# W2's Strassen block sums in DRAM and ScalarE squares, in one encoder layer

## Chip, cores and metric

The kernel runs on one core of a Trainium2 chip. The metric is the device time of one execution in microseconds (us); lower is better. The engines are named TensorE (PE in the profile; PEld are its weight loads), VectorE (DVE), ScalarE (ACT), GpSimd (POOL) and SyncE (SP, which only issues DMAs here).

## What is computed

One encoder layer on x of 2048 tokens by 1024 channels, all in float32. Two mixers read the same normalised input: dilated window attention (8 heads of 64) and a gated unit; a common output projection follows. Then comes the part that most of this document is about, the feed-forward network with hidden width 4096:

```python
x = x + rms_norm(mix, g_post_mix)
h = rms_norm(x, g_pre_ffn)
f = jnp.square(jax.nn.relu(h @ w_ff1)) @ w_ff2
return x + rms_norm(f, g_post_ffn)
```

w_ff1 is 1024 x 4096, w_ff2 is 4096 x 1024.

## The kernel before, in words

Every float32 product is made of three: each operand is split into a high part (a cast on ScalarE) and a low part (a subtraction on VectorE), and `mm3` (lines 92 to 94) adds low x high, high x low and high x high in PSUM. `split_sbuf` (lines 54 to 60) makes such a pair: line 59 is the cast, line 60 the subtraction; lines 56 and 57 are the same with a gain, for w_ff1.

The kernel has three stages. `stage1` norms x, projects it with w_in and writes the attention's operands to DRAM. `stage2` is the attention; it is left as it is. `stage3` has the output projection, in a loop over 16 token tiles written out by hand, and then the feed-forward network.

The network runs in 4 passes (`ps`) of 512 tokens, and in each pass over 8 groups (`g`, NG = 8) of 512 hidden channels. A group does this:

* First layer: 4 tiles f0 to f3 of 128 hidden channels by 512 tokens, 8 pieces of w_ff1 each (`ff1_first` does f0 and f1 together, `ff1_one` f2 and f3). `squares` (lines 934 to 940) applies Relu on ScalarE (line 937) and squares the result, in two halves of 256 tokens, on GpSimd (line 940).
* Second layer: Strassen's scheme in Winograd's form, 7 products instead of 8, over 2 x 2 blocks of tokens (256 each) by output columns (512 each) by hidden channels; the 512 hidden channels are two blocks, each of two tiles, p = 0 and p = 1. `operands` forms the four sums of hidden blocks on GpSimd (lines 1094, 1095, 1100, 1102) and the seven pairs fh, fl. p = 0 needs f0 and f2, p = 1 needs f1 and f3.
* `load2` (line 972) loads four tiles of 128 x 1024 of w_ff2, and `differences` (lines 983 to 985) and `second2` (line 1123) form its four block sums on GpSimd, anew in each pass; `first2` and `second2` make pairs wh, wl of the seven W2 operands. The first four operands (1, 2, 6, 5) have 8 buffers of their own; the other three (7, 3, 4) use the buffers of w_ff1's pieces after f3 is done.
* `ff2` runs the 7 products in the order of `CHAIN` for the row tiles m = 0 and 1. Sums that belong to several output blocks go on in the same PSUM bank: after product 1, VectorE adds the bank to `acc` (line 1154), and product 6 continues in this bank, so it has to wait for that addition. The order 1, 2, 6, 5, 7, 3, 4 uses the banks 1, 0, 1, 2, 1, 2, 1.
* `load1` loads and splits the next group's pieces of w_ff1.

TensorE, ScalarE, VectorE, GpSimd and SP each work through their own queue in order. Within the network and stage 1 that order is made by the scheduler of the language (program order is the priority among what is ready); in the loop of the output projection it is the written order for all five, and in stage 2 for TensorE and ScalarE. In that loop the loads of the first group's W2 tiles come at i = 13 and their differences at i = 16.

The first stage works with pools of buffers: x's tiles have the tag `xt` (4 buffers of 128 x 1024), the transposed tiles that go to DRAM the tag `ht` (2 buffers). `rstd_pow` (lines 98, 99) computes norm factors on GpSimd. `gates` is the gated unit for two token blocks; `prep` norms and transposes a tile of 128 tokens.

Of the kernel before, what the change touches and what calls it, by code (L numbers as in the profile page):

```python
# [9 lines left out]
F32 = mybir.dt.float32  # L10
F32R = mybir.dt.float32r
BF16 = mybir.dt.bfloat16
AF = mybir.ActivationFunctionType
ALU = mybir.AluOpType
# [3 lines left out]
P = 128  # L18
S = 2048
D = 1024  # L20
# [137 lines left out]
def stage1(tc, c, a, oh):  # L158
    nc = tc.nc
    with ExitStack() as ctx:  # L160
# [53 lines left out]
        def wload(col0):  # L214
            return [wpiece(col0, kc) for kc in range(8)]
# [108 lines left out]
        def gates(ws, hs, b0, w_next, between=None):  # L324

            v = do_zv(ws, hs[0])
            if between:
                between()
            w = wload(w_next)
            v2 = do_zv(ws, hs[1])  # L330
            do_sgu(v, b0)
            do_qk(w, hs[0], b0, c.qd, 0.125)
            do_sgu(v2, b0 + 1)
            return w


        hs = [new_h(), new_h()]
# [16 lines left out]
            nc.sync.dma_start(f32(c.vd[r0:r0 + P]), zeros)  # L354
        w = gates(wz, hs, 0, 0, consts)
        do_qk(w, hs[1], 1, c.qd, 0.125)
        w = wload(512)
        do_qk(w, hs[0], 0, c.kd, None)
        nh = [prep_all(2)]
        wz = wload(2048)  # L360
        do_qk(w, hs[1], 1, c.kd, None)
        nh.append(prep_all(3))
        hs = nh


        w = gates(wz, hs, 2, 0)
        zctx.close()
        do_qk(w, hs[1], 3, c.qd, 0.125)
        w = wload(512)
        for e in range(2):  # L370
            do_qk(w, hs[e], 2 + e, c.kd, None)
        w = wload(1024)
        do_v(w, hs[0], 2)
        c.wu = wload(1536)
        c.qk = c.qctx.enter_context(tc.tile_pool(name="s2q", bufs=2, side="right"))
        c.fk = c.fctx.enter_context(tc.tile_pool(name="s2fk", bufs=2, side="right"))
# [512 lines left out]
def stage3(tc, c, a, out):  # L889
# [4 lines left out]
    with ExitStack() as ctx:  # L894
# [39 lines left out]
        def squares(b, m, raw):  # L934

            raw[m] = fp.tile([P, 512], F32, name="rf", tag=f"rf{m}")
            nc.scalar.activation(raw[m], b, AF.Relu)  # L937
            for e in range(2):
                sl = raw[m][:, 256 * e:256 * e + 256]
                nc.gpsimd.tensor_tensor(sl, sl, sl, ALU.mult)  # L940

        def ff1_mm(b, h, ws, m, kc):
            wh, wl = ws[kc]
# [17 lines left out]
                    yield  # L961
            squares(b, m, raw)

        def load2(g):

            raws = []
            for p in range(2):
                two = []
                for e in range(2):
                    r = fp.tile([P, D], F32, name="w2r", tag="w2r", bufs=4)  # L970
                    k = 4 * g + 2 * e + p
                    nc.sync.dma_start(r, w2[k * P:(k + 1) * P, :])
                    two.append(r)
                raws.append(two)
            return raws

        def differences(raws):

            ts = []
            for r1, r2 in raws:  # L980
                t1 = fp.tile([P, 512], F32, name="t1", tag="t1", bufs=2)
                t2 = fp.tile([P, 512], F32, name="t2", tag="t2", bufs=2)
                nc.gpsimd.tensor_tensor(t1, r1[:, 512:], r1[:, :512], ALU.subtract)
                nc.gpsimd.tensor_tensor(t2, r2[:, 512:], t1, ALU.subtract)
                nc.gpsimd.tensor_tensor(r1[:, 512:], r2[:, 512:], r1[:, 512:], ALU.subtract)
                ts.append((t1, t2))
            return ts

        def start2(g):
            raws = load2(g)  # L990
            return raws, differences(raws)

        with ExitStack() as octx:
            orp = octx.enter_context(tc.tile_pool(name="s3r", bufs=4, side="right"))
# [23 lines left out]
            load_attn(nc, c, 1)  # L1018
            parts[0] = load_part(0)
            halves(0)  # L1020
            raws, ws0, raw0 = [], [], {}
            early = {7: 3, 8: 3, 9: 3, 11: 1, 12: 1, 13: 1, 14: 1, 15: 1}
            for i in range(18):
                old = 0 <= i - 1 < 16
                if 0 <= i - 3 < 4:
                    turned(xs[i - 3], h[0], h[1], i - 3)
                if i + 1 < 16:
                    halves(i + 1)
                if 0 <= i - 2 < 16:
                    nc.sync.dma_start(rows(i - 2), parts[i - 2])  # L1030
                    if i - 2 < 4:
                        rs2 = meansq(parts[i - 2])
                if old:
                    rs = meansq(parts[i - 1])
                if i < 16:
                    xs[i] = load_x(i)
                if i + 1 < 16:
                    parts[i + 1] = load_part(i + 1)
                if i == 7:
                    unit = ff1_first(h, ws0, raw0)  # L1040
                if i == 11:
                    unit = ff1_one(h, ws0, 2, raw0)
                if i == 13:
                    v0 = load2(0)
                if i == 16:
                    v0 = v0, differences(v0)
                for n in range(2):
                    if i < 16:
                        b = pm.tile([P, 512], F32, name="mo", tag="mm3")
                        ns = slice(n * 512, (n + 1) * 512)  # L1050
                        mh, ml = ops[i]
                        for kc in range(4):
                            mm3(nc, b, mh[:, kc, :], ml[:, kc, :], *c.wo[4 * n + kc], kc == 0, kc == 3)
                    for _ in range((early.get(i, 0) + 1 - n) // 2):
                        next(unit, None)
                    if old and n == 0:
                        r = parts[i - 1]
                        nc.vector.scalar_tensor_tensor(r, r, rs, gmix, ALU.mult, ALU.mult)
                        nc.vector.tensor_tensor(r, r, xs[i - 1], ALU.add)
                    if 0 <= i - 2 < 4 and n == 1:  # L1060
                        nc.scalar.activation(xs[i - 2], parts[i - 2], AF.Copy, scale=rs2)
                    if i < 16:
                        nc.vector.tensor_tensor(parts[i][:, ns], b, parts[i][:, ns], ALU.add)
                if i % 2 == 0 and i + 2 < 16:
                    product(nc, c, i // 2 + 1)
                    if i + 4 < 16:
                        load_attn(nc, c, i // 2 + 2)
                for _ in range(len(raws)):
                    ws0.append(piece_split(nc, c, raws.pop(0), c.gffn[:, len(ws0):len(ws0) + 1]))
                if 1 <= i < 5:  # L1070
                    raws = [piece_load(nc, c, w1[kc * P:(kc + 1) * P, 0:512]) for kc in range(2 * i - 2, 2 * i)]
# [4 lines left out]
        with ExitStack() as fctx:  # L1076
# [26 lines left out]
                op(3, a12)  # L1103
                op(4, a22)

            def w2op(pool, src):
                wh = pool.tile([P, 512], F32R, name="wh", tag="wh")
                wl = pool.tile([P, 512], F32R, name="wl", tag="wl")
                split_sbuf(nc, src, wh, wl)
                return wh, wl  # L1110

            def first2(v, ws):
                raws, ts = v
                for n in (1, 2, 6, 5):
                    for p in range(2):
                        src = {1: raws[p][0][:, :512], 2: raws[p][1][:, :512], 6: ts[p][1], 5: ts[p][0]}[n]
                        ws[n, p] = w2op(w2p, src)

            def second2(v, ws):
                raws, ts = v  # L1120
                for p in range(2):
                    r2 = raws[p][1]
                    nc.gpsimd.tensor_tensor(r2[:, :512], r2[:, :512], ts[p][1], ALU.subtract)
                for n in (7, 3, 4):
                    for p in range(2):
                        src = {7: raws[p][0][:, 512:], 3: raws[p][1][:, 512:], 4: raws[p][1][:, :512]}[n]
                        ws[n, p] = w2op(c.wp, src)

            def load1(g):
                return [piece(nc, c, w1[kc * P:(kc + 1) * P, g * 512:(g + 1) * 512], scale=c.gffn[:, kc:kc + 1])  # L1130
# [30 lines left out]
            for ps in range(4):  # L1161
# [33 lines left out]
                    return x1  # L1195

                for g in range(NG):
                    if ps == g == 0:
                        raw, v = raw0, v0
                    else:  # L1200
                        raw, v = {}, start2(g)
                    fs, w2s = {}, {}
                    first2(v, w2s)
                    if not ps == g == 0:
                        for _ in ff1_first(h, ws, raw):
                            pass
# [6 lines left out]
                    last = g == NG - 1  # L1213
                    if last and ps < 3:
                        nx = [next_in(i) for i in range(4)]
                    second2(v, w2s)
                    if not last or ps < 3:
                        ws = load1((g + 1) % NG)

# [40 lines left out]
def scratch(c, mk):  # L1260

    c.vd = mk("vd", [S + 2 * VPAD, NH, 2 * DH])
    c.qd = [[mk(f"qd{e}{m}", [P, S]) for m in range(4)] for e in range(2)]
    c.kd = [[mk(f"kd{e}{m}", [P, S]) for m in range(4)] for e in range(2)]
    c.hd = mk("hd", [16, P, 8, P], F32)
    c.sd = mk("sd", [16, P, 512], F32)
    c.sgd = mk("sgd", [16, P, 4, P], F32)
    c.part = mk("part", [S, D], F32)
    c.tab = mk("tab", [NH, 3 * 384], F32)
    c.bt = mk("bt", [NH, P, 3 * 384 + 1], F32)  # L1270
    c.od = mk("od", [512, S], F32)
    c.rd = mk("rd", [NH, S], F32)


# [62 lines left out]
```

## Time and profile before

| | us |
|---|---|
| median of 2 runs | 2805.06 (2803.39 to 2806.74) |
| the profiled execution, its time | 2790.99 |
| its span, first to last instruction | 2789.0 |
| TensorE busy (products) | 2452.9 (88%) |
| VectorE busy | 1850.3 (66%) |
| ScalarE busy | 1285.5 (46%) |
| GpSimd busy | 1134.3 (41%) |

Products are pipelined, so that a busy TensorE still contains time at the lower clock. Mean granted clock of the span: 0.924 of full speed. Stage 3's projection ends and the network's Strassen products begin at 1086.65.

### The profile page before, as it was taken

What the parts mean: (1) busy time and instruction counts of PE and PEld (TensorE: products, weight loads), DVE (VectorE), ACT (ScalarE), POOL (GpSimd) and SP (SyncE); (2) the same over time, 40 slices, a digit from 0 to 9 for tenths busy, and PEclk for the clock granted to TensorE, in tenths of its full rate; (3) what the DMA queues carried; (4) which work ended last, traced back from release to release, by engine and by line L of the source; (5) the groups of instructions that cost most, each with busy time, mean ns of one, the idle gap of its engine ahead of it and who ended that gap; (6) DMA issues with size and microseconds to landing.
All of it is one profiled execution on the core that took longest, in us unless ns stands there. A gap on an engine that the chain in (4) does not pass through costs nothing. (4 is left out here: it accounts for less than half of the span.)

```text
span 2789.0 us, 33978 instructions
## 1 busy us (share of the span) xinstructions
PE 2452.9 (88%) x11207; PEld 2002.8 (72%) x11207; DVE 1850.3 (66%) x3222; ACT 1285.5 (46%) x2837; POOL 1134.3 (41%) x1161
## 2 busy tenths in 40 slices
PE   8999999998998896888888898888789888888887
PEld 6787888887887675766766676676577667667766
DVE  4535335777665378677668767768776777776676
ACT  5334223776777344443345434335533434433433
POOL 4112006333321336454345435435534544543552
PEclk9999999999999998998998998899889899989989
DMA  7654557878866585222224222224322224322221
GB/s 257 198 185 133 177 166 216 206 184 198 192 152 175 179 280 212 84 83 77 83 71 164 83 76 91 68 83 151 99 78 69 91 73 143 107 74 84 74 86 42
DMA packets 232916, 365.51 MB, mean 131 GB/s; under 512 B 39201, under 2 KB 122660, under 8 KB 229668
## 3 DMA queue, kind: packets, MB, share of 16 engines
q1 hardware_dynamic: 207204, 349.44, 40.3%
q10 hardware_dynamic: 22976, 9.71, 1.3%
q0 software_dynamic: 2560, 4.20, 1.1%
q8 instruction: 88, 1.44, 0.2%
q14 instruction: 88, 0.72, 0.1%
HBM read 285.25 MB, written 82.74 MB: 132 GB/s over the span
## 5 line engine op out<-in xcount | busy, mean ns | idle before, releaser
L92 PE MATMUL g<-wl,fh 128*128 128x512 f32 x896 | 408.2, 457 | 193.9 <-DVE acc L1154 98.9
L93 PE MATMUL g<-wh,fl 128*128 128x512 f32 x896 | 404.8, 452 | 49.4 <-DVE fl L60 49.3
L60 DVE TENSOR_TENSOR fl<-rf,fh 128x256 fp32r<-128x256 f32 x320 | 262.0, 837 | 254.1 <-ACT fh L59 254.1
L940 POOL TENSOR_TENSOR rf<-rf 128x256 f32<-128x256 f32 x256 | 189.5, 765 | 587.7 <-ACT rf L937 587.7
L93 PE MATMUL f<-hh,wl 128*128 128x512 f32 x1024 | 399.1, 390 | 0.0
L94 PE MATMUL f<-hh,wh 128*128 128x512 f32 x1024 | 398.7, 389 | 0.0
L92 PE MATMUL f<-hl,wh 128*128 128x512 f32 x1024 | 398.5, 389 | 0.0
L94 PE MATMUL g<-wh,fh 128*128 128x512 f32 x896 | 395.5, 441 | 0.0
L92 PEld LDWEIGHTS g<-wl,fh 128*128 128x128 f32 x896 | 198.3, 222 | 269.7 <-DVE acc L1154 116.7
L57 DVE SCALAR_TENSOR_TENSOR wl<-wraw,gain,wh 128x512 fp32r<-128x512 f32 x328 | 309.5, 956 | 99.8 <-ACT wh L56 96.9
L56 ACT ACTIVATE wh<-wraw,gain 128x512 fp32r<-128x512 f32 x328 | 232.5, 721 | 273.7 <-DMA wraw<-in_w_ff_dram 119.6
L60 DVE TENSOR_TENSOR wl<-w2r,wh 128x512 fp32r<-128x512 f32 x320 | 267.2, 868 | 111.7 <-ACT wh L59 111.4
L1154 DVE TENSOR_TENSOR acc<-g,acc 128x512 f32<-128x512 f32 x416 | 271.5, 680 | 43.8 <-PE g L94 41.4
L93 PEld LDWEIGHTS g<-wh,fl 128*128 128x128 f32 x896 | 199.6, 223 | 104.0 <-DVE fl L60 61.7
L94 PEld LDWEIGHTS g<-wh,fh 128*128 128x128 f32 x896 | 198.8, 222 | 45.1
L93 PEld LDWEIGHTS f<-hh,wl 128*128 128x128 f32 x1024 | 192.3, 188 | 41.2 <-DVE wl L57 1.3
L92 PEld LDWEIGHTS f<-hl,wh 128*128 128x128 f32 x1024 | 192.3, 188 | 40.0
L94 PEld LDWEIGHTS f<-hh,wh 128*128 128x128 f32 x1024 | 192.3, 188 | 39.9
L937 ACT ACTIVATE rf<-f 128x512 f32<-128x512 f32 x128 | 75.8, 594 | 284.0 <-PE f L94 281.4
L59 ACT CAST fh<-rf 128x256 fp32r<-128x256 f32 x320 | 126.4, 406 | 154.6 <-POOL rf L940 76.3
L588 ACT ACTIVATE p<-p,m 128x256 f32<-128x256 f32 (+2 forms) x384 | 173.9, 458 | 32.5 <-DVE m L558 15.7
L59 ACT CAST wh<-w2r 128x512 fp32r<-128x512 f32 x320 | 177.5, 616 | 8.5 <-PE mo L94 2.2
(179 smaller groups left out, 5161.1 us busy)
## 6 DMA issues: line engine op xcount, KB each, us to landing
wraw<-in_w_ff_dram SPq DMA_DIRECT2D x256, 256.0 KB, 2.7
w2r<-in_w_ff_dram SPq DMA_DIRECT2D x128, 512.0 KB, 3.5
wraw<-in_w_in_dram SPq DMA_DIRECT2D x72, 256.0 KB, 2.9
xt<-in_x_dram SPq DMA_DIRECT2D x32, 512.0 KB, 7.6
v<-vd SPq DMA_DIRECT2D x40, 256.0 KB, 5.9
v<-vd SPq DMA_DIRECT2D x8, 1088.0 KB, 7.1
hd<-ht ACTq DMA_DIRECT2D x16, 512.0 KB, 4.5
vd<-vt SPq DMA_DIRECT2D x16, 512.0 KB, 3.2
```

The source lines that it names most:

```text
L56: nc.scalar.activation(hi, src, AF.Copy, scale=scale)
L57: nc.vector.scalar_tensor_tensor(lo, src, scale, f32(hi), ALU.mult, ALU.subtract)
L59: nc.scalar.copy(hi, src)
L60: nc.vector.tensor_tensor(lo, src, f32(hi), ALU.subtract)
L92: nc.tensor.matmul(out, lhsT=lh, rhs=rl, start=start, stop=False, skip_group_check=on)
L93: nc.tensor.matmul(out, lhsT=ll, rhs=rh, start=False, stop=False, skip_group_check=on)
L94: nc.tensor.matmul(out, lhsT=lh, rhs=rh, start=False, stop=stop, skip_group_check=on)
L588: nc.scalar.activation(p[:, at + lo:at + hi], p[:, at + lo:at + hi], AF.Exp, bias=o.m[:, br, cc:cc + 1], scale=-1.0, accum_out=o.dn[:, br, ...
L937: nc.scalar.activation(raw[m], b, AF.Relu)
L940: nc.gpsimd.tensor_tensor(sl, sl, sl, ALU.mult)
L1154: nc.vector.tensor_tensor(av, b, av, ALU.add)
```

## The change

It has two parts. First, the four block sums of W2 are formed once, in stage 1: `sums` is called 16 times (once for each group and half p), loads two tiles of w_ff2 through GpSimd's DMA queue into buffers `xt`, makes four subtractions of 128 x 512 on GpSimd and writes the four sums to a new DRAM tensor `td[i]` with three DMAs. In the network, `load2` loads the seven operands as pieces of 128 x 512, three straight from w_ff2 and four from `td`, through SP's queue and 10 buffers; the differences are gone. Second, the squares are done on ScalarE behind Relu. The early loads of the first group move to i = 12 to 15.

```diff
@@ stage1
+            else:
+                sums()
             w = wload(w_next)
             v2 = do_zv(ws, hs[1])
+            sums()
             do_sgu(v, b0)
+            sums()
             do_qk(w, hs[0], b0, c.qd, 0.125)
...
+        def sums():
+            i = todo.pop(0)
+            g, p = divmod(i, 2)
+            rs = []
+            for e in range(2):
+                r = wk.tile([P, D], F32, name="wr2", tag="xt", bufs=4)
+                k = 4 * g + 2 * e + p
+                nc.gpsimd.dma_start(r, w2[k * P:(k + 1) * P, :])
+                rs.append(r.rearrange("r (n c) -> r n c", n=2))
+            r1, r2 = rs
+            t = wk.tile([P, 8, P], F32, name="wt2", tag="ht").rearrange("r (n k) c -> r n (k c)", n=2)
+            nc.gpsimd.tensor_tensor(t[:, 0, :], r1[:, 1, :], r1[:, 0, :], ALU.subtract)
+            nc.gpsimd.tensor_tensor(t[:, 1, :], r2[:, 1, :], t[:, 0, :], ALU.subtract)
+            nc.gpsimd.tensor_tensor(r1[:, 1, :], r2[:, 1, :], r1[:, 1, :], ALU.subtract)
+            nc.gpsimd.tensor_tensor(r2[:, 0, :], r2[:, 0, :], t[:, 1, :], ALU.subtract)
+            nc.gpsimd.dma_start(c.td[i][:, 0:2, :], t)
+            nc.gpsimd.dma_start(c.td[i][:, 2, :], r1[:, 1, :])
+            nc.gpsimd.dma_start(c.td[i][:, 3, :], r2[:, 0, :])
...
         w = gates(wz, hs, 0, 0, consts)
         do_qk(w, hs[1], 1, c.qd, 0.125)
+        sums()
+        sums()
...
         do_v(w, hs[0], 2)
+        while todo:
+            sums()
         c.wu = wload(1536)
@@ stage3
-                nc.gpsimd.tensor_tensor(sl, sl, sl, ALU.mult)
+                nc.scalar.activation(sl, sl, AF.Square)
...
+        def load2(g, ns):
             raws = []
+            for n in ns:
+                for p in range(2):
+                    r = fp.tile([P, 512], F32, name="w2r", tag="w2r", bufs=10)
+                    k = 4 * g + p + (0 if n == 1 else 2)
+                    if n < 4:
+                        src = w2[k * P:(k + 1) * P, 512 * (n == 3):512 * (n == 3) + 512]
+                    else:
+                        src = c.td[2 * g + p][:, {5: 0, 6: 1, 7: 2, 4: 3}[n], :]
+                    nc.sync.dma_start(r, src)
+                    raws.append(r)
             return raws
-        def differences(raws):
...
-                if i == 13:
-                    v0 = load2(0)
-                if i == 16:
-                    v0 = v0, differences(v0)
+                if 12 <= i < 16:
+                    v0 += load2(0, ((1, 2, 6, 5)[i - 12],))
...
+            def split2(pool, raws, ns, ws):
+                for j, raw in enumerate(raws):
+                    wh = pool.tile([P, 512], F32R, name="wh", tag="wh")
+                    wl = pool.tile([P, 512], F32R, name="wl", tag="wl")
+                    split_sbuf(nc, raw, wh, wl)
+                    ws[ns[j // 2], j % 2] = wh, wl
...
-                    first2(v, w2s)
+                    split2(w2p, v, first, w2s)
...
-                    second2(v, w2s)
+                    split2(c.wp, load2(g, (7, 3, 4)), (7, 3, 4), w2s)
```

The other calls of `sums` stand behind the projections and norms of stage 1, one or two at a place.

## Rows read from the trace of the kernel before

**Rows 1.** Stretch: us, busy us (x instructions) of five engines, clock, DMA share, GB/s
```profile
1090.00:2789.00 1699.00, 1453.20 (x5758) 1157.90 (x5758) 1238.85 (x1637) 733.66 (x1408) 807.29 (x806) 0.90 0.27 90
```

**Rows 2.** TensorE timeline: start, duration; in brackets idle before and its releaser
```profile
1198.36 0.50 PE L92 MATMUL g<-wl,fh 128*128 128x512 f32 x1 [1.95 <-ACT fh L59]
...
1411.96 0.50 PE L92 MATMUL g<-wl,fh 128*128 128x512 f32 x1 [1.95 <-ACT fh L59]
...
2596.78 0.50 PE L92 MATMUL g<-wl,fh 128*128 128x512 f32 x1 [1.95 <-ACT fh L59]
2598.84 0.80 PE L93 MATMUL g<-wh,fl 128*128 128x512 f32 x1 [1.56 <-DVE fl L60]
...
2608.25 0.80 PE L92 MATMUL g<-wl,fh 128*128 128x512 f32 x1 [3.37 <-DVE acc L1154]
```

**Rows 3.** The same timeline, end of the slow stretch, and the first layer
```profile
2610.98 0.51 PE L92 MATMUL g<-wl,fh 128*128 128x512 f32 x1
...
2622.03 0.39 PE L92 MATMUL f<-hl,wh 128*128 128x512 f32 x1
...
2641.75 0.39 PE L92 MATMUL f<-hl,wh 128*128 128x512 f32 x1
```

**Rows 4.** Short stretches with their clock (third number from the end)
```profile
2438.52:2440.52 2.00, 1.93 (x5) 1.55 (x6) 1.50 (x4) 1.00 (x4) 2.00 (x3) 0.50 0.76 260
2404.55:2406.55 2.00, 0.00 (x1) 0.00 (x1) 2.00 (x5) 0.05 (x1) 0.00 (x0) 1.00 0.00 0
```

**Rows 5.** Timeline of ScalarE, the same group
```profile
2591.71 0.41 ACT L59 CAST fh<-rf 128x256 fp32r<-128x256 f32 x1 [0.17 <-POOL rf L1102]
2592.02 2.70 ACT L59 CAST wh<-w2r 128x512 fp32r<-128x512 f32 x5
2594.63 0.58 ACT L937 ACTIVATE rf<-f 128x512 f32<-128x512 f32 x1
...
2596.32 0.41 ACT L59 CAST fh<-rf 128x256 fp32r<-128x256 f32 x1 [0.50 <-POOL rf L940]
```

**Rows 6.** Timeline of GpSimd, the same group
```profile
2595.29 2.02 POOL L940 TENSOR_TENSOR rf<-rf 128x256 f32<-128x256 f32 x2 [1.22 <-ACT rf L937]
...
2600.21 1.45 POOL L984 TENSOR_TENSOR t<-w2r,t 128x512 f32<-128x512 f32 x1
```

**Rows 7.** Timeline of VectorE, the same group
```profile
2605.85 1.75 DVE L57 SCALAR_TENSOR_TENSOR wl<-wraw,gain,wh 128x512 fp32r<-128x512 f32 x1
2607.52 2.47 DVE L1154 TENSOR_TENSOR acc<-g,acc 128x512 f32<-128x512 f32 x4
...
2620.94 0.74 DVE L57 SCALAR_TENSOR_TENSOR wl<-wraw,gain,wh 128x512 fp32r<-128x512 f32 x1
...
2634.19 0.43 DVE L60 TENSOR_TENSOR fl<-rf,fh 128x256 fp32r<-128x256 f32 x1 [7.52 <-ACT fh L59]
```

**Rows 8.** Groups by line from 1053 us on: count, busy us, mean ns, idle before
```profile
L940 POOL TENSOR_TENSOR rf<-rf 128x256 f32<-128x256 f32 x252 | 186.6, 765 | 585.8 <-ACT rf L937 585.8
L59 ACT CAST fh<-rf 128x256 fp32r<-128x256 f32 x320 | 126.4, 406 | 154.6 <-POOL rf L940 76.3 <-POOL rf L1102 48.3 <-POOL rf L1100 28.3
...
L983 POOL TENSOR_TENSOR t<-w2r 128x512 f32<-128x512 f32 x64 | 99.2, 1549 | 16.8 <-DMA w2r<-in_w_ff_dram 16.8
```

**Rows 9.** Start of the network: timelines of TensorE and ScalarE
```profile
1086.65 1.19 PE L92 MATMUL g<-wl,fh 128*128 128x512 f32 x2 [14.70 <-ACT fh L59]
...
1076.90 0.62 ACT L59 CAST wh<-w2r 128x512 fp32r<-128x512 f32 x1 [1.05 <-POOL w2r L985]
```

**Rows 10.** Stage 1: a stretch, a GpSimd row, GpSimd DMA issues (ns min/median/max)
```profile
200.00:300.00 100.00, 95.92 (x449) 79.64 (x448) 50.11 (x82) 42.98 (x75) 25.01 (x30) 0.97 0.44 144
...
194.52 2.38 POOL L200 TENSOR_TENSOR ht<-hh,hl 128x1024 f32<-128x1024 f32 x1 [63.06 <-DVE hl L84]
...
L648 POOL DMA_DIRECT2D od<-acc x16: 802/864/1071, 522.9 to 915.6; - x16
```

**Rows 11.** Waits of the SP queue from 1100 us: total, times, longest
```profile
SPq L972 <- DVE wl L60: 674.1, 120, 14.9
```

More of the change, by code (lines that the diff above doesn't have):

```diff
@@ L334, in gates @@
             return w
+        w2 = a["w_ff2"][0]
+        todo = list(range(16))
+        def sums():
[16 more added lines that the diff above has]
+            nc.gpsimd.dma_start(c.td[i][:, 3, :], r2[:, 0, :])
         hs = [new_h(), new_h()]
@@ L362, in stage1 @@
         nh.append(prep_all(3))
+        sums()
         hs = nh
@@ L368, in stage1 @@
         do_qk(w, hs[1], 3, c.qd, 0.125)
+        sums()
         w = wload(512)
@@ L371, in stage1 @@
             do_qk(w, hs[e], 2 + e, c.kd, None)
+            sums()
+            sums()
         w = wload(1024)
         do_v(w, hs[0], 2)
+        while todo:
+            sums()
         c.wu = wload(1536)
@@ L962, in ff1_one @@
             squares(b, m, raw)
-        def load2(g):
+        def load2(g, ns):
             raws = []
[L967 to L974, printed above, removed]
-            return raws
-        def differences(raws):
[L979 to L991, printed above, removed]
+            for n in ns:
[8 more added lines that the diff above has]
+                    raws.append(r)
+            return raws
         with ExitStack() as octx:
@@ L1020, in stage3 @@
             halves(0)
-            raws, ws0, raw0 = [], [], {}
+            raws, ws0, raw0, v0 = [], [], {}, []
             early = {7: 3, 8: 3, 9: 3, 11: 1, 12: 1, 13: 1, 14: 1, 15: 1}
@@ L1104, in operands @@
                 op(4, a22)
[L1106 to L1127, printed above, removed]
+            def split2(pool, raws, ns, ws):
[4 more added lines that the diff above has]
+                    ws[ns[j // 2], j % 2] = wh, wl
             def load1(g):
@@ L1197, in stage3 @@
                 for g in range(NG):
[L1198 to L1201, printed above, removed]
+                    first = (1, 2, 6, 5)
+                    raw, v = (raw0, v0) if ps == g == 0 else ({}, load2(g, first))
                     fs, w2s = {}, {}
-                    first2(v, w2s)
+                    split2(w2p, v, first, w2s)
                     if not ps == g == 0:
@@ L1271, in scratch @@
     c.od = mk("od", [512, S], F32)
+    c.td = [mk(f"td{i}", [P, 4, 512], F32) for i in range(16)]
     c.rd = mk("rd", [NH, S], F32)
```

## Prediction

> **What bounds the kernel now.** I read the busy times by stage first, then TensorE's idle stretches in order of time, then what the other engines did in one of these stretches, and last the groups by line. The first view tells where there is anything to win: from 1090 us to the end, 1699 us, TensorE is busy for 1453 and its granted clock is 0.90 [rows 1]. That is the feed-forward network, 32 groups (4 passes over tokens, 8 slices of the hidden width).
>
> In that stretch the idle rows repeat like a stamp. A group has three stalls: 1.95 us for an fh from ScalarE, 1.56 us for the fl that belongs to it, then 3.37 us for an accumulation on VectorE [rows 2]. From the stall at 1198.36 to its like at 1411.96 four groups pass, so a group takes 53.4 us [rows 2]. Undisturbed, TensorE starts a product every 0.227 us: 87 of them lie between 2622.03 and 2641.75 [rows 3]. A group has 96 products of the first layer and 84 of Strassen's scheme (7 products x 2 row tiles x 2 K halves x 3 terms), so 180 x 0.227 = 40.8 us. **12.6 us of each group are lost**: about 7 idle, and the rest mostly to the clock, which stands at 0.50 after the pair of stalls [rows 4], that is at 1.2 instead of 2.4 GHz: the 21 products from 2598.84 to 2610.98 took 8.8 us without the stall among them, 0.42 each, 4.0 us too long [rows 2, 3].
>
> Why the stalls come: the last tile of the hidden layer ends near 2591.4, but its Relu starts at 2594.63. ScalarE works in order and had waited for the last operand of the half before (from GpSimd), then did five W2 casts [rows 5]. Then GpSimd squares for 2.02 us, and only then can ScalarE cast fh at 2596.32 [rows 5, 6]. Behind that, GpSimd puts a W2 difference of 1.45 us in the middle of the operands [rows 6]. VectorE runs slow at the same time: its split of w1 takes 1.75 us beside GpSimd and 0.74 us where GpSimd idles [rows 7], and the accumulation that frees a PSUM bank stands in its queue behind these splits, until 2608 [rows 7]. So GpSimd is not the busiest engine, but it is what ends last, twice in each group.
>
> **The change, part by part.**
>
> *GpSimd in the network.* It loses the squares (252 x 0.765 us) and four sorts of W2 operations, of which the first has 64 x 1.55 us [rows 8]. Per group that is 8 x 0.765 = 6.1 and 8 x about 1.5 = 12 us. What is left are 8 operand sums of about 0.9 us.
>
> *ScalarE.* It gains 8 squares of 128x256 per group. A cast of that shape took 0.406 us [rows 8], so 8 x 0.41 = 3.2 us. I cost this at nothing in throughput: ScalarE is busy 734 of 1699 us [rows 1], and 32 x 3.2 = 102 us more leaves it under half. On the path two squares of 0.82 us stand where GpSimd had 2.02 and a handover.
>
> *The new group.* I count from 2591.3, when the Strassen products begin. TensorE has 15 products (3.4 us) before it needs the operand made from the last hidden tile, at 2594.7. With ScalarE's order unchanged, Relu starts some 0.4 us earlier than now, 2594.2, squares end at 2595.6, fh at 2596.0, fl at 2596.5: one stall of 1.4 to 1.9 us. If the casts no longer stand before Relu, squares end at 2592.9 and there is no stall. I take 0.9. Next is the accumulation. If squares end at T, four operand sums (3.7 us), cast, fl of 0.43 [rows 7], one split of 0.74 and the accumulation of about 0.65 put the bank free at T + 5.9; TensorE arrives at T + 4.1 in the first case (stall 1.8) and 0.7 us too early in the second. I take 1.3. A single stall leaves the clock alone: TensorE was idle through 2404.55 to 2406.55 and the clock stayed 1.00 [rows 4]. Two stalls four microseconds apart are not shown, so I bound the clock's cost by today's 4.0 us and by nothing, and take 1.0, nearer to the idle row. Loss per group: 0.9 + 1.3 + 1.0 = 3.2, with ends at 0.7 (a little is always late) and 1.8 + 1.8 + 4.0 = 7.6. **A group then takes 44.0 instead of 53.4 us.**
>
> *Sum for the network.* The 24 groups in the middle of passes save 24 x 9.4 = 226 us. The 8 at the ends of passes have other waits too (norms, transposes of the next pass); I give them two thirds, 8 x 6.3 = 50. Ahead of the first group TensorE waits 14.70 us for fh, while ScalarE's queue waits for a W2 difference on GpSimd [rows 9]. All six differences leave that place; the Relu, squares and first casts need some 4 us, so I take 11 saved. Together 287 us.
>
> *W2 pieces through DRAM.* A group's W2 loads go from 4 of 512 KB to 14 of 256 KB, 2.1 to 3.7 MB, on SP's queue, with 10 slots. The share of the DMA engines in this stage is 0.27 [rows 1], so bandwidth hides it. Casts and splits of W2 keep their number. The queue is a rival below.
>
> *The first stage.* The sums are made 16 times: two loads and three stores on GpSimd's DMA queue and four subtractions of 128x512. A DMA issue of GpSimd took 0.80 to 1.07 us [rows 10], a W2 difference 1.55 us [rows 8], so 16 x (5 x 0.9 + 4 x 1.55) = 171 us of GpSimd. There is room: GpSimd is 0.25 busy in 200 to 300 us and had stood idle for 63 us before 194.5 [rows 10]. The bytes are 16 x 2.1 = 33.6 MB; at 144 GB/s for a share of 0.44 [rows 10] they want about 103 us of all engines, spread over some 300 us, and the share rises to about 0.8. What is at risk: the norm factors of the token blocks are GpSimd instructions in the same order, now behind subtractions that wait for a load, and the loads take x's buffers. Bounds: a gain is excluded, since nothing is removed there; from nothing to 40 us (the last three or four sums after the stage's end at 11 us each). I take 6, nearest to the idle row.
>
> In that stage a DMA issue next to a busy VectorE is shown only by the 0.80 to 1.07 us of the rows. The Trainium skill (SBUF — State Buffer, "SBUF: two separate sides") warns of this very thing: descriptors written by GpSimd wait while VectorE runs an instruction through both ports, 3100 instead of 620 ns. By that figure, an estimate, 80 issues would cost 80 x 3.1 = 248 us, and the sums would spill out of the stage; the rows show no such issue.
>
> **Sum.** 2790.99 - 287 + 6 = 2510 us for the profiled execution. The median shown, 2805.06, is 14 us above that execution, so 2524 us.
>
> **Rivals.**
>
> 1. *Everything hides.* Casts leave the place before Relu, 0.7 us lost per group: 24 x 11.9 = 286, the ends 8 x 8 = 64, 14 at the start: 2805 - 364 + 6 = 2447. For it: the scheduler places instructions afresh, and the pieces are loaded earlier. Against: in-order ScalarE has done casts first in each group.
>
> 2. *The clock keeps falling.* Two stalls of 1.8 us remain in each group and the clock still drops: 7.6 lost, a group of 48.4. 24 x 5.0 + 8 x 3.3 + 5 = 151: 2805 - 151 + 6 = 2660. For it: 1.95 and 1.56 us were enough for the drop [rows 2, 4]. Against: these stand one product apart, the new ones nine or more.
>
> 3. *The sums outlast the first stage*, because issues are slow or the loads wait: the next stage's buffers come free 40 us late. 2524 + 34 = 2558.
>
> 4. *SP's queue becomes the bound: slower than before.* SP already waits 674.1 us in 120 waits, 5.6 us each, until VectorE frees a W2 slot [rows 11]. With 14 loads on 10 slots, four per group wait so, 22.5 us, and the w1 loads queue behind them. A group would take 44 + 22.5 = 66.5 us, 13 more than now: 2805 + 32 x 13 = 3220. It decides from the point when w1 pieces come later than the first layer eats them, one per 6 products (1.4 us). Against: the first layer runs without one gap today [rows 3], and the slots come free during the Strassen half.
>
> 5. *The time doesn't follow* (the change does not do what it says): the DRAM sums are read but the waits are set by VectorE's backlog, whose work is unchanged. Two stalls of today's size in each group, less a little: within 2%, about 2770. Against: VectorE is busy 1239 of 1699 us [rows 1] and part of that is slowing by GpSimd.
>
> **How the numbers follow.** Forecast 0.55, rival 1 0.15, rival 2 0.17, rival 3 0.05, rival 4 0.03, rival 5 0.05. A measurement of this kernel tells about 2% (56 us) from no change. Faster: 0.55 + 0.15 + 0.17 + 0.05 = 0.92; same 0.05; slower 0.03. The range reaches rival 1 below and rival 2 above with some room for the first stage: 2435 to 2680.
>
> **What would show it.** Right: GpSimd some 250 us busy after 1090 us instead of 807 [rows 1]; ScalarE about 100 us more; the three stalls shrunk to one or two below 2 us; mean granted clock in the network 0.97 or more; VectorE's busy time there some 10% lower with the same count; the stall ahead of the first group under 5 us. Wrong: first-layer products waiting for w1 splits (rival 4); clock at 0.50 in every group (rival 2); TensorE idle around 220 us or at the start of the second stage by more than 10 us (rival 3); accumulation waits of 3 us or more (rival 5).

## The result, and the profile after

The kernel after takes **2639.72 us** (2637.97 to 2641.47, 2 runs) where the kernel before takes 2805.06: a ratio of 0.941, interval 0.937 to 0.945. It is faster, inside the range of 2435 to 2680, and 116 us above the forecast of 2524. The profiled execution took 2641.47 us, 149.5 less than that of before.

The stretches of the kernel after, columns as in [rows 1]. 420.94 us is where the first stage ended in the kernel before; the other limits are landmarks in TensorE's timeline (the attention's first score product, the output projection's first product, the first Strassen product):

```profile
0.00:420.94 420.94, 347.46 (x1541) 280.99 (x1541) 170.72 (x233) 135.06 (x231) 206.65 (x237) 0.92 0.69 236
420.94:485.81 64.87, 63.26 (x278) 51.86 (x277) 22.26 (x32) 19.85 (x31) 8.31 (x8) 1.00 0.63 195
485.81:1017.97 532.16, 484.26 (x3118) 426.89 (x3119) 331.33 (x1199) 338.39 (x1056) 182.47 (x183) 0.94 0.71 180
1017.97:1158.63 140.66, 116.84 (x514) 94.19 (x512) 96.33 (x115) 57.75 (x114) 43.57 (x58) 0.95 0.89 276
1158.63:2639.00 1480.37, 1354.56 (x5760) 1087.13 (x5760) 1017.21 (x1644) 794.82 (x1662) 244.58 (x308) 0.97 0.41 137
```

The kernel before, by its own landmarks of the same kind:

```profile
0.00:420.94 420.94, 398.98 (x1817) 326.73 (x1818) 173.89 (x265) 156.01 (x262) 83.46 (x101) 0.99 0.57 186
420.94:941.40 520.46, 480.34 (x3119) 421.52 (x3120) 330.97 (x1199) 337.77 (x1056) 181.25 (x183) 0.95 0.74 184
941.40:1086.65 145.25, 119.18 (x513) 96.17 (x512) 103.27 (x119) 57.84 (x111) 58.98 (x69) 0.93 0.76 264
1086.65:2789.00 1702.35, 1454.39 (x5760) 1158.37 (x5760) 1242.20 (x1640) 733.87 (x1409) 810.64 (x809) 0.90 0.27 90
```

Two things happened. The network fell from 1702 to 1481 us with the same 5760 products: GpSimd went from 811 to 245 us, the clock from 0.90 to 0.97, VectorE's busy time from 1242 to 1017 us. But by 420.94 us, where the kernel before had done its first stage, TensorE had made 1541 products instead of 1817, and the stage ended 65 us later (485.81). **The change gives 221 us in the network and takes 72 back before it**, and that is the 149 us between the two spans (2789.0 and 2639.7). Of the 72, 65 are the first stage; the attention took 12 longer (532 instead of 520) and the projection 5 less.

In the network the stamp of [rows 2] is smaller. TensorE's timeline, first groups of the first pass:

```profile
1158.63 1.19 PE L92 MATMUL g<-wl,fh 128*128 128x512 f32 x2 [10.49 <-ACT fh L59]
...
1209.38 0.49 PE L92 MATMUL g<-wl,fh 128*128 128x512 f32 x1 [1.03 <-ACT fh L59]
1215.69 0.50 PE L92 MATMUL g<-wl,fh 128*128 128x512 f32 x1 [2.00 <-DVE acc L1159]
1256.02 0.50 PE L92 MATMUL g<-wl,fh 128*128 128x512 f32 x1 [1.02 <-ACT fh L59]
1262.33 0.50 PE L92 MATMUL g<-wl,fh 128*128 128x512 f32 x1 [2.06 <-DVE acc L1159]
...
1437.78 0.50 PE L92 MATMUL g<-wl,fh 128*128 128x512 f32 x1 [1.02 <-ACT fh L59]
```

From 1209.38 to 1437.78 lie five groups, so a group takes 45.7 us (53.4 before, 44.0 forecast). The stalls of 1.95 and 3.37 us are now 1.03 and 2.04; that of 1.56 us for fl is 0.30. Why the second is 2.04 is seen on VectorE, in a later group:

```profile
1677.13 1.41 DVE L57 SCALAR_TENSOR_TENSOR wl<-wraw,gain,wh 128x512 fp32r<-128x512 f32 x2
1678.46 3.13 DVE L1159 TENSOR_TENSOR acc<-g,acc 128x512 f32<-128x512 f32 x5
```

Two splits of w1 stand ahead of the addition that frees the bank. The first stall is ScalarE's: the five W2 casts of [rows 5] still stand ahead of Relu, and only GpSimd's 2.02 us and its handovers are gone:

```profile
1668.22 2.70 ACT L59 CAST wh<-w2r 128x512 fp32r<-128x512 f32 x5
1670.82 0.59 ACT L974 ACTIVATE rf<-f 128x512 f32<-128x512 f32 x1
...
1671.82 0.72 ACT L977 ACTIVATE rf<-rf 128x256 f32<-128x256 f32 x2
1672.44 0.70 ACT L59 CAST fh<-rf 128x256 fp32r<-128x256 f32 x2
```

In the first stage the long stalls are new; TensorE's timeline:

```profile
99.02 1.44 PE L121 MATMUL tb<-ohs,rb 33*8 33x384 f32 x2 [8.25 <-DMA ohs<-in_onehot_dram]
141.76 0.27 PE L321 MATMUL tpb<-ident,br 8*128 8x8 f32 x1 [24.50 <-DVE wsl L84]
...
325.41 0.58 PE L92 MATMUL sg<-vl,wsh 128*128 128x256 f32 x1 [11.71 <-DVE vl L60]
```

The longest can be followed through the queues of two engines. GpSimd and VectorE, same stretch:

```profile
112.44 0.30 DVE L277 BATCH_NORM_AGGREGATE mv<-st 128x2 f32<-128x6 f32 x2
136.01 1.67 DVE L280 TENSOR_SCALAR z<-z,mv,rs 128x512 f32<-128x512 f32 x1 [23.28 <-POOL rs L99]
...
141.02 0.68 DVE L84 TENSOR_TENSOR wsl<-tpw,wsh 128x512 fp32r<-128x512 f32 x1
...
123.88 0.56 POOL L352 DMA_DIRECT2D wr<-in_w_ff_dram  x1 [8.32 <-DMA td<-wr]
132.65 1.25 POOL L357 TENSOR_TENSOR wt<-wr,wt 128x512 f32<-128x512 f32 x1 [8.21 <-DMA wr<-in_w_ff_dram]
133.99 0.22 POOL L98 TENSOR_SCALAR rs<-mv 128x1 f32<-128x1 f32 x1
```

The statistics for a norm factor lay ready at 112.7. GpSimd took them up at 133.99, because the queue in front waited 8.32 us for a store to free a row buffer and 8.21 us for W2's load. VectorE stood at line 280 for 23.28 us, with wsl behind it, which TensorE wanted next: 24.50 us idle for two instructions of under a microsecond. The 8.25 us hang on the same queue: the load that TensorE waited for stood on SP behind a store that had waited 17.4 us for a memset on GpSimd, and the memset came behind sums.

What GpSimd waited for up to 490 us, for the sums' transfers alone (total us, times, longest):

```profile
POOL wr L352 <- DMA td<-wr: 25.5, 9, 8.3
POOL wt L357 <- DMA wr<-in_w_ff_dram: 21.3, 6, 8.2
POOL wt L356 <- DMA wr<-in_w_ff_dram: 9.3, 6, 3.6
```

Together 56 us; the 64 subtractions themselves took 90 us and the 80 DMA issues 45.

### The profile page after: what moved, and what is told of

Same layout as the page of the kernel before. It is cut to its first block, busy times and chain, and to the rows that moved or that the text cites. A ratio compares the mean times of both kernels' runs of the same rounds, so it can differ in the third digit from the quotient of the medians.

```text
span 2639.7 us, 34693 instructions
## 1 busy us (share of the span) xinstructions
PE 2366.4 (90%) x11207; PEld 1941.1 (74%) x11207; DVE 1637.9 (62%) x3222; ACT 1345.9 (51%) x3093; POOL 685.6 (26%) x793
## 4 chain that ended last, share of the span: by engine, by line
PE 33%; DVE 8%; ACT 7%; POOL 3%; DMA 3%; issue 2%; ACTq 0%; SPq 0%; DVEq 0%; POOLq 0%
PE f L94 6%; PE f L92 6%; PE f L93 6%; PE g L92 5%; PE g L94 5%; PE g L93 5%; DVE fl L60 4%; ACT wh L59 3%; DVE wl L57 2%; ACT rf L977 1%; DVE wl L60 1%; ACT rf L974 1%; DMA w2r<-td 1%; POOL rf L1121 1%; POOL rf L1123 1%
## 5 line engine op out<-in xcount | busy, mean ns | idle before, releaser
L92 PE MATMUL g<-wl,fh 128*128 128x512 f32 x896 | 368.6, 412 | 104.7 <-DVE acc L1159 51.6
L60 DVE TENSOR_TENSOR fl<-rf,fh 128x256 fp32r<-128x256 f32 x320 | 164.9, 541 | 367.4 <-ACT fh L59 367.4
L93 PE MATMUL g<-wh,fl 128*128 128x512 f32 x896 | 364.5, 407 | 11.0 <-DVE fl L60 10.8
L94 PE MATMUL g<-wh,fh 128*128 128x512 f32 x896 | 360.6, 403 | 0.0
L1115 POOL TENSOR_TENSOR s<-rf 128x256 f32<-128x256 f32 x64 | 47.3, 740 | 1071.6 <-ACT rf L977 1064.5
L57 DVE SCALAR_TENSOR_TENSOR wl<-wraw,gain,wh 128x512 fp32r<-128x512 f32 x328 | 251.5, 793 | 114.2 <-ACT wh L56 110.8
L60 DVE TENSOR_TENSOR wl<-w2r,wh 128x512 fp32r<-128x512 f32 x448 | 291.6, 690 | 11.3 <-ACT wh L59 8.8
L59 ACT CAST wh<-w2r 128x512 fp32r<-128x512 f32 x448 | 255.4, 617 | 73.6 <-PE g L94 61.2
L93 PEld LDWEIGHTS g<-wh,fl 128*128 128x128 f32 x896 | 174.7, 195 | 57.1 <-DVE fl L60 22.2
L94 PEld LDWEIGHTS g<-wh,fh 128*128 128x128 f32 x896 | 175.1, 195 | 36.6
```

What stands on the lines that cost most here:

```text
L57: nc.vector.scalar_tensor_tensor(lo, src, scale, f32(hi), ALU.mult, ALU.subtract)
L59: nc.scalar.copy(hi, src)
L60: nc.vector.tensor_tensor(lo, src, f32(hi), ALU.subtract)
L92: nc.tensor.matmul(out, lhsT=lh, rhs=rl, start=start, stop=False, skip_group_check=on)
L93: nc.tensor.matmul(out, lhsT=ll, rhs=rh, start=False, stop=False, skip_group_check=on)
L94: nc.tensor.matmul(out, lhsT=lh, rhs=rh, start=False, stop=stop, skip_group_check=on)
```

## The experiments

The first four are each half of the change alone, the sums as pure extra work, and the change with the sums taken out.

**Squares alone** (the kernel before with one line changed):

```diff
-                nc.gpsimd.tensor_tensor(sl, sl, sl, ALU.mult)
+                nc.scalar.activation(sl, sl, AF.Square)
```

> The kernel before, with the squares on ScalarE and nothing else. Theory (each of two parts shortens a different stall of a group): the fh stall falls from 1.95 + 1.56 to about 1.5 us, the accumulation stall of 3.4 to 4.4 us stays at 2 to 3.5 because W2 differences still stand among the operand sums; a group of 47 to 50 us, the first stage as before, 2805 - 32 x 5 = about 2645 us (2630 to 2700). Rival (the W2 differences are what holds GpSimd, squares alone change nothing): group above 52 us, time above 2760.

Measured 2738.3 us, ratio 0.978 (0.974 to 0.983): a miss by 93, outside the theory's range and short of the rival's. A group took 51.2 us; the wait for fh fell to 1.03 us, but GpSimd still put W2's differences among the operands, another wait of 1.3 us for an fl came in, and the accumulation stall was 4.37 us.

**W2's sums alone** (the kernel after with that line put back):

> The changed kernel with the squares back on GpSimd. Theory: the squares again stand between Relu and fh (1.2 to 2 us instead of 0.7), group 47 to 50 us, and the first stage is 65 us longer as in the changed kernel: 2805 - 32 x 4.5 + 65 = about 2726 us (2680 to 2760). Rival (the squares are what matters in the group): group 52 us or more, time above 2800.

Measured 2691.5, ratio 0.962 (0.957 to 0.966), in its range; a group took 47.1 us. So most of the network's gain is W2's part; the squares add 1.4 us a group once the differences are gone.

**Sums made and not used** (the first stage of after, the network of before):

> The kernel before plus the 16 sums in the first stage, whose result nobody reads; the network is that of before. Theory (the sums alone make the first stages longer): network starts 65 to 75 us later, time 2870 to 2885. Rival (the later start comes from the early W2 loads or from the network's new buffers): within 20 us of 2805.

Measured 2868.1, ratio 1.025 (1.021 to 1.029), 2 us below its range. Against 2798.1 for the kernel before, measured beside it, the sums cost 70 us. The first Strassen product came 71 us later, 64 of them in the first stage.

**No sums** (the kernel after with an empty list of sums; the network reads columns of w_ff2 in their place, so this run leaves the sums' values out):

```diff
-        todo = list(range(16))
+        todo = []
...
-                        src = c.td[2 * g + p][:, {5: 0, 6: 1, 7: 2, 4: 3}[n], :]
+                        src = w2[k * P:(k + 1) * P, 512 * (n % 2):512 * (n % 2) + 512]
```

> The changed kernel without the sums: the first stage is that of before, and the network loads w_ff2's own columns in place of the four sums (so the second layer's product is left out of the comparison: part of W2's operands is replaced). Theory: all of the stage's cost goes, the group stays at 45.7 us: 2640 - 65 to 72 = 2568 to 2575. Rival (cost elsewhere, or reads of the new DRAM tensors cost in the network): above 2610.

Measured 2571.2, ratio 0.919 (0.914 to 0.924), in its range; the first Strassen product came at 1090.49 instead of 1158.63, and the groups were as in after. **The sums cost 68 to 70 us by both runs.** The attention took 532 us without sums too, so its 12 us are not theirs; what they are is open (one trace of each kernel). What in the sums costs the time, and whether it has to, was the next question; beside it, what is left in the network.

**Sums behind the norm factors:**

```diff
         def sums():
+            with tc.issue_after(c.fence):
+                sums_()
```

with `c.fence` the last norm factor of the gated unit's second half, or of the rows of block 3. Two of the 16 sums lose their place in it and come at the end of the stage.

> After, with each pair of subtractions of W2's blocks issued on GpSimd only behind the norm factors of the batch's second half (and, in the group without gated unit, behind those of the next rows); nothing left out. Theory (GpSimd's queue in order: a subtraction that waits for W2's load or for a store holds up the norm factors behind it, and with them VectorE, then TensorE): the first stage gets back most of its 70 us, first Strassen product before 1115, total 2575 to 2600; the waits of 24.5 us behind wsl and of 8.25 us behind the one-hot load are gone. Rival a (W2's 8 MB and the sums' stores compete for transfer time, or for the buffers, with the stage's own loads): the same bytes move, so the stage stays within 15 us of after and the total is 2625 or more. Rival b (GpSimd itself has too little room for the subtractions): the work collects at the stage's end and the total is 2600 to 2640, with TensorE waiting there.

Measured 2621.9, ratio 0.938 (0.935 to 0.941): the theory's time was missed by 22, and the time is in the range of rival b. The stalls of 24.50 and 8.25 us were gone and the first Strassen product came at 1137.84, 21 us earlier, but others came in their place. TensorE, ScalarE, GpSimd, and what SP issued meanwhile:

```profile
185.41 0.80 PE L92 MATMUL mm<-hl,wh 128*128 128x512 f32 x1 [13.74 <-DVE e L87]
...
393.00 0.79 PE L92 MATMUL mm<-wl,hh 128*128 128x512 f32 x1 [11.69 <-DVE wl L57]
406.75 0.80 PE L92 MATMUL mm<-wl,hh 128*128 128x512 f32 x1 [10.83 <-DVE e L84]
...
171.40 1.06 ACT L186 ACTIVATE jk<-xt 128x1024 bf16<-128x1024 f32 x1 [11.20 <-DMA xt<-in_x_dram]
...
385.21 1.26 POOL L140 TENSOR_TENSOR xl<-fr,xh 128x512 fp32r<-128x512 f32 x1
...
386.49 0.33 SPq L132 DMA_DIRECT2D fr<-hd  x1
386.92 7.66 SPq L261 DMA_DIRECT2D kd<-e  x8
```

The first: a load of x stood on SP until a store of the sums freed a buffer that both use (11.5 us), ScalarE waited 11.20 us for these rows, and the emptying of TensorE's banks stood behind that. So the shared buffers of rival a have a part in it (W2 is 16.8 MB, not the 8 named there). The others: a load for the second stage waited 36.7 us on SP until GpSimd, behind sums, had split an earlier piece (line 140 at 385.21); the K stores behind that load waited too, and with them the buffers TensorE's banks empty into.

**The addition first:** the splits of the next W1 pieces, and with them those of W2's last three operands, are traced behind the second accumulation.

```diff
-                    split2(c.wp, load2(g, (7, 3, 4)), (7, 3, 4), w2s)
-                    if not last or ps < 3:
-                        ws = load1((g + 1) % NG)
+                    rest = load2(g, (7, 3, 4))
+                    def pieces():
+                        split2(c.wp, rest, (7, 3, 4), w2s)
+                        if not last or ps < 3:
+                            c.ws = load1((g + 1) % NG)
...
+                            if j == 1:
+                                pieces()
```

> After, with the splits of the next W1 pieces traced behind the second accumulation of a group instead of ahead of it; nothing left out. Theory (the wait of 2.04 us in every group is the second accumulation of product 1 standing behind two splits of 1.41 us on VectorE): the wait falls to about 0.7 us, the interior group from 45.7 to 44.3, 28 groups give 38 us, total 2595 to 2610. Rival a (VectorE is full and another wait takes its place): the group stays above 45.2 and the total above 2625. Rival b (the clock falls less often as well, once only one wait of over 1 us is left in a group): the group comes to 43.5 or less and the total to 2580 or less.

Measured 2582.9, ratio 0.924 (0.921 to 0.927), faster than the theory's range and 3 us short of rival b's. The stall fell to the theory's 0.7 us, and what rival b adds held too: the clock stayed up (1.00 from 1250 to 2480 us). A group took 43.7 us.

```profile
1250.95 0.49 PE L92 MATMUL g<-wl,fh 128*128 128x512 f32 x1 [1.03 <-ACT fh L59]
1255.92 0.50 PE L92 MATMUL g<-wl,fh 128*128 128x512 f32 x1 [0.71 <-DVE acc L1159]
```

**Relu first too:** the same `pieces`, its casts kept behind the squares of f3, and product 5 ahead of 6 in `CHAIN`.

```diff
+                    c.sq = nc.cur_bb.bb.instructions[-1]
...
+                        with tc.issue_after(c.sq):
+                            split2(c.wp, rest, (7, 3, 4), w2s)
```

> After, with product 5 ahead of product 6 in the chain and the second casts of W2 kept behind the squares of the fourth unit, so that neither Relu nor an accumulation stands behind casts or splits; nothing left out. Theory (what is left of the group's loss is order on ScalarE, five casts of 2.70 us ahead of Relu, and on VectorE, 1.41 us ahead of the accumulation): both waits fall below 0.6 us, the group comes to 43.0 to 44.0, total 2565 to 2595. Rival (products 6 and 7 now follow each other in one bank, and the splits that were ahead of the operands stand ahead of the accumulation of 6): a wait of 1 to 3 us appears ahead of product 7, the group stays at 45 to 46.5 and the total within 25 us of 2640.

Measured 2557.9, ratio 0.914 (0.912 to 0.916), 7 us below its range. Both stalls left the Strassen half, and a group took 42.5 us (1265.10 to 1435.26 for four); a single wait of 1.2 us is left, of the next first layer for the last accumulations.

**Fence and order together:**

> The first run and the third of this call together; nothing left out. Theory: stage 1 and the network are apart, so the gains add: if the fence gives 50 and the order 55, total 2525 to 2545, the forecast's size. Rival (either did not give what it should): the total says by how much, as the sum of what the two single runs show.

Measured **2529.2 us, ratio 0.904 (0.902 to 0.906)**, the best of all, faster than both kernels. Against the 0.941 of the kernel after, the fence alone gave 0.003, less than the intervals, though its span is 21 us shorter; the order alone gave 0.027, both 0.037. That the total lies in its range is luck in the parts: 50 and 55 us were expected, 18 and 82 measured, and beside the order the fence gave 29.

The next two take the sums apart; in both the network reads columns of w_ff2, as without sums. **Transfers alone** (the 64 subtractions left out, three stores of what was loaded):

> After, with the 64 subtractions left out: the same loads of W2 and the same three stores a row block, of what was loaded, from GpSimd's queue; the network reads four column blocks of W2 itself, as in the run without sums (2571). Theory (what costs the first stage 68 us is GpSimd, SP and the shared row buffers waiting for the sums' transfers to come and go): at least 45 us of it stay, total 2615 to 2645. Rival (it is GpSimd's own time, 64 subtractions of 1.3 us in its queue ahead of the norm factors): less than 25 us stay, total 2570 to 2595.

Measured 2593.8, ratio 0.928 (0.924 to 0.933): the rival's range. First Strassen product at 1114.20, 24 us later than without sums, though GpSimd waited 76 us for the sums' transfers here, more than the 56 in the kernel after.

**Subtractions alone** (64 of the same size, of rows that are on the chip anyway; one of the four lines shown):

```diff
-            nc.gpsimd.tensor_tensor(t[:, 0, :], r1[:, 1, :], r1[:, 0, :], ALU.subtract)
+            nc.gpsimd.tensor_tensor(t[:, 0, :], f32(hs[1][0][:, 0, :]), f32(hs[1][0][:, 1, :]), ALU.subtract)
```

> After, with the sums' loads and stores left out: the same 64 subtractions on GpSimd, of two rows that are on the chip anyway, at the same places of the program; the network reads four column blocks of W2 itself. Theory of the transfers: the first stage is within 15 us of that without sums, total 2570 to 2586. Rival (GpSimd's own time): 40 us or more of the 68 stay, total 2610 to 2640.

Measured 2629.7, ratio 0.941 (0.937 to 0.945): the rival again, 62 us of stage 1 (first Strassen product at 1152.90) without one transfer. **My theory that the transfers' waits alone were the cost fell:** without transfers most of it can come back. GpSimd, ScalarE and TensorE:

```profile
62.34 1.55 POOL L350 TENSOR_TENSOR wt<-hh 128x512 f32<-128x512 f32 x1 [0.15 <-DMA hd<-ht]
...
87.05 2.48 POOL L353 TENSOR_TENSOR wt<-hh,wt 128x512 f32<-128x512 f32 x2
89.61 0.51 POOL L98 TENSOR_SCALAR rs<-ms 128x1 f32<-128x1 f32 x2
90.80 2.19 ACT L191 ACTIVATE xt<-xt,rs 128x1024 f32<-128x1024 f32 x2 [21.75 <-POOL rs L99]
...
95.03 0.80 PE L92 MATMUL mm<-wl,hh 128*128 128x512 f32 x1 [20.89 <-DVE vt L84]
...
329.77 0.58 PE L92 MATMUL sg<-vl,wsh 128*128 128x256 f32 x1 [33.98 <-DVE vl L60]
```

With nothing to wait for, the scheduler put 20 subtractions in a row, 27 us, ahead of a pair of norm factors; ScalarE waited 21.75 us for these (line 191) with the emptying of TensorE's banks behind it, and TensorE lost 20.89. At 329.77 it lost 33.98 in the same way. So it is the place in GpSimd's queue, and the queue can be held by its own work or by a transfer. The 24 and 62 us are not parts of the 68: this order is another than that of after, where no 20 subtractions stand in a row and 16.5 of the 21.3 us ahead of the norm factor at 133.99 are waits for transfers.

**The queues' order mended:** the last version, with the second stage's load behind the K stores and two sums moved past the second rows' loads.

```diff
-        c.raw = fload(nc, c, c.unit[1])
+        with tc.issue_after(c.kst):
+            c.raw = fload(nc, c, c.unit[1])
```

> The run of the fence and the order of the network together (2529), with the load of the second stage's unit kept behind the last K stores on SP's queue, and with the two sums that stood ahead of the second rows' loads moved behind the second gated unit; nothing left out. Theory (the waits of 12.40, 11.43 and 10.78 us that the fence left are a row load that waits for the sums' buffers, and stores on SP held up behind a load that waits for GpSimd): these waits fall below 4 us each, total 2495 to 2510. Rival (the sums need that time on the transfers or on GpSimd wherever they are put): the waits come back at other places of the first stage or at its end, total 2520 or more.

Measured 2533.1, ratio 0.906 (0.903 to 0.910), no better than 2529.2. The three waits named there (12.40, 11.43 and 10.78 us in the run before it) went, but there was a new one of 6.49 us, and one of 27.46 at the stage's end:

```profile
445.31 0.77 PE L92 MATMUL f<-wl,xh 128*128 128x512 f32 x1 [27.46 <-issue]
...
442.87 0.59 ACT L83 CAST vt<-mm 128x512 fp32r<-128x512 f32 x1 [46.83 <-DMA vd<-vt]
```

Now V's stores stood on SP behind loads that waited for GpSimd. The rival holds: of the places tried in this stage none was free; a wait taken from one came back at another. Giving them buffers of their own, another engine or a later stage was not tried, so it is not shown that the sums need this time wherever they stand.

## Why the prediction was right, and where it was not

*Direction and mechanism: right.* GpSimd went to 245 us in the network ("some 250"); three stalls became two of about 2 us or less; VectorE got faster with nearly the same count, by more than forecast (18% for "some 10%"): its low parts of `rf`, 837 ns before, now take 541. Those of `s`, made while GpSimd forms the operands, went from 707 to 828. ScalarE's 248 squares took 410 ns each, as the casts did, 102 us added up; its busy time in the stretch rose by 61 only (records that overlap count once there).

*The time in the range: in part luck.* The range's top, 2680, was rival 2 with "some room for the first stage"; what filled it was the first stage, which no rival had at this size, and only a part of rival 2.

*"I take 6" for the first stage: the step that failed.* It measured 68 to 70, beyond its bound of 40; by the stretches above it is 59 (65 found, 6 taken) of the 131 us by which the profiled executions differ from the forecast's sum (281 forecast, 149.5 found). The risk was named, norm factors behind subtractions that wait for a load, and the trace after shows it, but it was priced by the idle row, 63 us of GpSimd [rows 10]. That row says how much time the queue has, not whether it is free when a norm factor comes: a block of sums ahead of one took 21 us in the kernel after, and 27 us in the run of subtractions alone. The bound counted work left over at the end, 11 us a sum; but the last sum was issued at 405.64, 80 us before the stage ended. A block of sums ahead of each batch of norm factors, with VectorE and TensorE behind it, would have been nearer; no run tests that count. Nor was it the price of GpSimd's own work: 171 us were taken, and subtractions and issues took 135. Most issues took 0.53 to 0.61 us, the longest 0.80, where [rows 10] had 0.80 to 1.07. The 3.1 us of the Trainium skill that I had set beside it (SBUF — State Buffer, "SBUF: two separate sides") showed in none of the 80. The page gives that figure for a transfer beside a VectorE copy; the issues of 0.55 and 0.54 us at 138.82 and 139.36 ran beside two-input products (138.61), so they do not test it.

*The group, "44.0": 45.7, too small by 1.7*, 41 us in 24 groups. Terms: first stall 0.9 taken, 1.03 and 0.30 found; accumulation 1.3 taken, 2.04 found, since two splits stood in front of it and not "one split of 0.74"; clock 1.0 taken, 0.8 found; 0.7 of the loss of 4.9 stays unassigned. The run with the accumulation first shows that term directly: a group of 43.7.

Another 12 us are the attention's, which the forecast left as it was; their cause stays open.

*The ends of passes, "8 x 6.3 = 50":* the network's 221 less 24 x 7.7 leaves 36, 14 too few. *The start, "11 saved":* 14.70 became 10.49, so 4, and the sign "under 5 us" did not come: taking the differences away left the casts, Relu and squares in ScalarE's order, and the sum without GpSimd's waits was not "some 4 us".

The rivals: 1 needed Relu ahead of the casts, which the scheduler did not do by itself; the run that made it do so reached 42.5 a group. Rival 2 came half: the clock falls in about every other group. Rival 3 had the right place, and loads that wait are a part of the cause; but the sums did not outlast the stage. Of 4 and 5 nothing was seen.

## What to carry to other kernels

An engine that is 25% busy is not free for background work if it also makes small things that others wait for: what counts is the longest block that can come to stand in front of one of them, here 21 us in the kernel after and 27 in the run of subtractions alone, ahead of an instruction of 0.2 us. Look for that block when you price moved work, waits for transfers included, and see where a store or load on a shared queue passes the wait on.
When an engine is taken off the path, the next loss is often order and not work: moving two splits of 0.7 us and five casts behind what TensorE waited for, with two products exchanged, gave 0.027 of the time, some 75 us and more than the first stage had lost, with every instruction still there.

## What the runs showed of the chip

The same stalls did not always bring the clock down. In the kernel after, two groups with the same stalls (1.03 and about 2.0 us, 6.3 us apart) differ behind the second:

```profile
1215.69:1220.00 4.31, 4.31 (x12) 3.46 (x13) 3.02 (x5) 1.77 (x4) 0.00 (x0) 0.62 0.32 115
...
1262.33:1267.00 4.67, 4.67 (x21) 3.86 (x22) 4.53 (x8) 2.66 (x6) 0.00 (x0) 1.00 0.42 144
```

0.62 is a mix of the two levels, 1.2 and 2.4 GHz: eight products started 0.43 us apart, then the pace was 0.23 again. So groups of 46.6 and 45.0 us come about equally often. With stalls of 1.03 and 0.71 us, in the run with the accumulation first, the clock was 1.00 behind both and each group took 43.7: of the 2.0 us saved, 1.3 are the shorter wait, and the rest is about what the clock had cost (0.8).
